# Freeing the normalised input tile by tile, earlier scores, and another split of the PSUM banks in a hybrid conv and stick-breaking attention layer

## The chip, the core and the metric

The kernel runs on one core of a Trainium2 chip. The core has five engines that run side by side and wait for each other through semaphores: TensorE (PE in the profile, its weight loads as PEld), VectorE (DVE), ScalarE (ACT), GpSimd (POOL) and SyncE (SP, which here issues the transfers between HBM and the on-chip memory). Matmul results land in PSUM, which has eight banks of 128 partitions by 512 floats; everything else sits in SBUF. The metric is the device time of one execution in microseconds (us).

## The reference

One layer over 2048 positions of 1024 channels:

```python
shift, scale, gate = jnp.split(mod[:, None, :], 3, axis=-1)
h = rms_norm(x, norm_g[l]) * (1.0 + scale) + shift
u = h @ w_in[l]
glu_in, gate_a, q, k, v, gate_b, m_a, m_b = jnp.split(u, IN_SPLITS, axis=-1)
y_a = conformer_conv_branch(glu_in, gate_a, w_dw[l], b_dw[l], ln_g[l], ln_b[l], w_conv_out[l])
q = head_rms_norm(q.reshape(bsz, seq, SB_HEADS, SB_HEAD_DIM), q_gain[l])
k = head_rms_norm(k.reshape(bsz, seq, SB_HEADS, SB_HEAD_DIM), k_gain[l])
o = stick_breaking_attention(q, k, v).reshape(bsz, seq, D_SB)
y_b = (o * jax.nn.silu(gate_b)) @ w_sb_out[l]
y = jax.nn.sigmoid(m_a) * y_a + jax.nn.sigmoid(m_b) * y_b
x = x + gate * (y @ w_out[l])
```

In the attention (8 heads of 64) a position t weighs an earlier position s by `beta[t,s]` times the product of `1 - beta[t,j]` over the positions between them, with `beta = sigmoid(q.k / 8)`. There is no softmax: the weights come from a running product along the keys.

## The kernel before

**Layout.** The host reverses the positions, so that the running product goes forward. The 2048 positions are four chunks of 512 (`NCH`, `CH`). Channels lie on the 128 partitions, so 1024 channels are eight tiles (`KC`). Each value that enters a matmul is held as a rounded high part and the remainder, and a product is three matmuls, `mm3` (high x high, high x low, low x high). A float32 weight piece of 128 x 1024 is loaded and split into its two parts by `split_into` (L99): two transfers of 512 columns through the tile `wl`, a copy on ACT, and a subtraction for the low part on POOL, or on DVE when so asked. `load_piece` puts the parts into the pool `wpa`, which has two buffers of each.

**Stages.** First the normalised input h is built for the four chunks, in the order `ORDER` = 3, 2, 1, 0, and kept in SBUF as 16 tiles a chunk (eight high, eight low; `h_tiles`, L173); the projections, the convolution and its LayerNorm follow. Queries, keys, values, gates and the branch results z (`za` from the convolution, `o` from the attention) go through HBM. Then comes the attention stage, from about 776 us on, which this document is about. The last stage multiplies z by `w_cs` (both branch projections), merges with the gates to y (`y_tiles`), multiplies by `w_out` (`out_tile`), chunk by chunk.

**The attention stage.** It runs over 80 units (h, rc, g): head, chunk of queries and chunk of keys from the diagonal on, ten for each head, four of them diagonal. One iteration of the loop takes the scores of unit u and the output of the unit before it, p, interleaved. For each of four blocks of 128 queries, Z(qb) (`z_stage`, L931) does this:

- PE: two matmuls into a PSUM bank of the pool `pz` (two banks). On a diagonal the columns that aren't needed are left out, so they are 512, 384, 256 and 256 wide.
- ACT: a sigmoid into the SBUF tile `w` (L953), then the sigmoid of the negative score over the bank itself (L954).
- DVE: the running product along the keys, a scan into `sc` (L958, or L962 on a diagonal), which reads the bank.
- POOL: the product of `w` and the shifted scan (L965), on a diagonal also a mask (L967).

The tile `w` has seven buffers (L952). For p, T(kb) (`av_stage`, L974) transposes the weights of a block of keys, one transpose for each query block (four, on a diagonal kb+1), into a PSUM tile `pT`; ACT copies its high part to `thi` (L991), DVE takes the low part `tlo` (L992), both with a priority 30 instructions ahead of their place. For the smallest diagonal block, kb = 0, 128 columns of `thi` and `tlo` are set to zero on POOL (L988, L989). AV(kb) (`av_mm`, L996) multiplies both by the values into a bank of the pool `pa` (two banks), which adds up over a row group (h, rc). When the row group is complete, ACT and DVE read the two halves of the bank out into `oc` (L1005, L1006).

Between these, `others(q, half)` puts in **fill**: the 13 remaining blocks of the merge gates, each for four chunks, in steps of one `mm3` (416 steps, `NF`, 14 of them ahead of the loop). A quarter q is a quarter of an iteration, numbered through the stage; `due` spreads the fill nearly evenly up to quarter `LAST` = 302. An output of the fill goes through a sigmoid into the tile `fsg` (two buffers, shared with `oc`) and to HBM.

The order of PE in this stage is that of the program (`pin`). On the other engines, and on SP, a scheduler fixes the order when the kernel is built, by priority, which is the place in the program, and by its own estimates.

**The changeover.** At quarter 302 the fill has ended. `hst.close()` gives back the tiles of h of all chunks as whole pools, and the pools `wr` and `yp` take their place. z of chunk 0 is loaded and split there (`load_za`, L1025, `load_zb`, L1035, through the `io` tiles), and `wcs[1]` is loaded. From quarter 307 on (`LAST + LAG`) each half quarter also does one step of `y_tiles` for chunk 0, which loads the pieces `wcs[2]` and on, two tiles ahead of their use, with the low part on DVE. The stage ends with quarter 323.

The order inside an iteration, before:

```python
Z(0); others(4 * n_, 0); av_mm(*held); others(4 * n_, 1)
Z(1); T(3); others(4 * n_ + 1, 0); T(2); others(4 * n_ + 1, 1)
Z(2); others(4 * n_ + 2, 0); AV(3); T(1); AV(2); T(0); Z(3)
others(4 * n_ + 2, 1); others(4 * n_ + 3, 0); others(4 * n_ + 3, 1); AV(1)
```

`held` is AV(0) of the iteration before.

Of the kernel before, what the change touches and what calls it, by code (L numbers as in the profile page):

```python
# [19 lines left out]
P = 128  # L20
# [31 lines left out]
def trunk_kernel(  # L52
# [115 lines left out]
    wpa = ctx.enter_context(tc.tile_pool(name="wpa", bufs=2))  # L168
    hst = ExitStack()
    hp = hst.enter_context(tc.tile_pool(name="hp", bufs=1))  # L170
    hT_ = {}

    def h_tiles(pool, g):  # L173
        hT_[g] = tuple([pool.tile([P, CH], F32R, name=f"h{p}{kc}_{g}") for kc in range(KC)]
                       for p in ("hi", "lo"))

    def hT(g):
        return hT_[g]
# [706 lines left out]
    with ExitStack() as s2:  # L885
        at = s2.enter_context(tc.tile_pool(name="at", reuse_waits="tile", bufs=1, side="right"))
        pd = s2.enter_context(tc.tile_pool(name="pd2", reuse_waits="tile", bufs=2, space=PSUM))
        pz = s2.enter_context(tc.tile_pool(name="pz", reuse_waits="tile", bufs=2, space=PSUM))
        pw = s2.enter_context(tc.tile_pool(name="pw", reuse_waits="tile", bufs=2, space=PSUM))
        pa = s2.enter_context(tc.tile_pool(name="pa", reuse_waits="tile", bufs=2, space=PSUM))  # L890
# [9 lines left out]
        def filler():  # L900

            rest = blocks[NEARLY:]
            nxt = load_piece(wpa, w_in[rest[0][0]])
            for i, (blk, dst) in enumerate(rest):
                whi, wlo = nxt
                for g in range(NCH):
                    ps = pd.tile([P, CH], F32, tag="pd", name="pd")
                    rhi, rlo = hT(g)
                    for kc in range(KC):
                        s = slice(kc * P, (kc + 1) * P)  # L910
                        mm3(ps, whi[:, s], wlo[:, s], rhi[kc], rlo[kc], kc == 0, kc == KC - 1)
                        if kc == KC - 1:
                            sg = at.tile([P, CH], F32, tag="fsg", name="fsg", bufs=2)
                            nc.scalar.activation(out=sg, in_=ps, func=AF.Sigmoid)
                            nc.sync.dma_start(dst[g], sg)
                            if g == 0 and i + 1 < len(rest):
                                nxt = load_piece(wpa, w_in[rest[i + 1][0]])
                        yield
# [55 lines left out]
        def av_stage(h, rc, g, kb, v_):  # L974
            diag = g == rc
            s_ = st[h, rc]
            if diag and kb == 3:
                s_["av"] = pa.tile([P, CH], F32, tag="av", name="av")
            av = s_["av"]
            n = (kb + 1) * P if diag else CH  # L980
            pT = pw.tile([P, CH], F32, tag="pT", name="pT")
            for qb in range(n // P):
                tr(pT[:, qb * P:(qb + 1) * P],
                                    s_["w"][g, qb][:, kb * P:(kb + 1) * P], ident)
            thi = at.tile([P, CH], F32R, tag="thi", name="thi", bufs=2)
            tlo = at.tile([P, CH], F32R, tag="tlo", name="tlo", bufs=2)
            if n == P:
                nc.gpsimd.memset(f(thi[:, P:2 * P]), 0.0)  # L988
                nc.gpsimd.memset(f(tlo[:, P:2 * P]), 0.0)  # L989
            with tc.high_priority(offset=30):  # L990
                nc.scalar.copy(out=thi[:, :n], in_=pT[:, :n])  # L991
                nc.vector.tensor_tensor(out=tlo[:, :n], in0=pT[:, :n], in1=f(thi[:, :n]),  # L992
                                        op=ALU.subtract)
            return max(n, 2 * P), av, thi, tlo
# [15 lines left out]
        wcs, wo = {}, {}  # L1010

        def resident(pool, src, name):
            hi = pool.tile([P, 1024], F32R, name=name + "h")
            lo = pool.tile([P, 1024], F32R, name=name + "l")
            split_into(src, hi, lo, nc.vector)
            return hi, lo

# [7 lines left out]
        def load_za(ch):  # L1025
            z = []
            for kc in range(JC):
                t = yp.tile([P, 2, CH], F32R, tag=f"za{kc}", name=f"za{kc}")
                o = io("n")
                nc.sync.dma_start(o, za_d[kc][ch])  # L1030
                split_z(o, t)
                z.append(t)
            return [t[:, 0, :] for t in z], [t[:, 1, :] for t in z]

        def load_zb(ch):  # L1035
            z = []
            for kc in range(JC):
                t = yp.tile([P, 2, CH], F32R, tag=f"zb{kc}", name=f"zb{kc}")
# [7 lines left out]
            return [t[:, 0, :] for t in z], [t[:, 1, :] for t in z]  # L1046

        def y_tiles(ch, za, zb, psum, y):

            for j in range(KC):  # L1050
                for i in range(2, min(KC, j + 3)):
# [42 lines left out]
        LAST = 4 * len(units) - 18  # L1094
        PRE = 14
        LAG = 5
# [15 lines left out]
        for n_, u in enumerate(units + [None]):  # L1112
# [15 lines left out]
            def others(q, half):  # L1128

                nonlocal nf, ny, ygen, wr, yp  # L1130
                while nf < (int(due[2 * q + half + 1] + 0.001) if q < LAST else NF):
                    next(fill)
                    nf += 1
                if q == LAST - 8 and not half:
                    wcs[0] = load_piece(wpa, w_cs[0])
                if q == LAST and not half:
                    hst.close()
                    wr = s3.enter_context(tc.tile_pool(name="wr", reuse_waits="tile", bufs=1))
                    yp = s3.enter_context(tc.tile_pool(name="yp", reuse_waits="tile", bufs=1))
                    with tc.high_priority(offset=0):  # L1140
                        za = load_za(0)
                        zb = load_zb(0)
                        wcs[1] = load_piece(wpa, w_cs[1])
                    ygen = y_tiles(0, za, zb, lambda n: psum(n), y)
                if q >= LAST + LAG:
# [16 lines left out]
            T(1)  # L1162
            AV(2)
            T(0)
            Z(3)
# [13 lines left out]
    with s3:  # L1179
# [3 lines left out]
        for ch in range(NCH):  # L1183
# [8 lines left out]
            for j in range(KC):  # L1192
                if ch == 0:
                    wo[j] = resident(wr if j == 0 else wor, w_out[j], f"wo{j}")
# [50 lines left out]
```

## Time and profile before

| | us |
|---|---|
| median of three runs | 1851.29 (1850.65 to 1852.08) |
| the profiled execution | 1852.87 |
| its span, first to last instruction | 1850.9 |
| attention stage in it | about 776 to 1520 |

The profile is one execution, recorded by the hardware. "Busy" of PE counts overlapping matmuls once, so a full share doesn't mean that PE is at its peak; the distance from one matmul's start to the next one's does. In a group's row stand the line, engine, operation, the tiles written and read, the shapes and the count, then the busy time, the mean length in ns and, behind the bar, the engine's idle time right before them with what ended it. In the timeline stand start, length, engine, line and operation, and in brackets the idle time before it. L118 is the helper through which every matmul goes, L123 that of the transposes; there the tiles tell them apart: `z` scores, `pT` transposes, `av` output, `pd` fill, `p` merge.

### The profile page before, as it was taken

The numbers are of one execution on the slowest core, as the hardware profiler recorded it, in microseconds if no ns is written. First come the engines' busy times: TensorE is split into PE (matmuls) and PEld (weight loads), VectorE is DVE, ScalarE is ACT, GpSimd is POOL, SyncE is SP. The second block draws the span as 40 slices with busy tenths as digits, with TensorE's granted clock in tenths as the row PEclk, the third lists the DMA queues.
The fourth block names the chain that finished last, engine by engine and source line by source line (L and its number), as shares of the span: only waits on it lengthen the run. The fifth ranks groups of instructions, "written<-read, shape, count | busy, mean of one in ns | idle before, by whom it ended". The sixth has DMA issues, their size and how long they took to land.

```text
span 1850.9 us, 27230 instructions
## 1 busy us (share of the span) xinstructions
PE 1781.9 (96%) x9612; PEld 1511.5 (82%) x9612; DVE 1232.4 (67%) x1696; ACT 825.4 (45%) x1896; POOL 668.8 (36%) x883
## 2 busy tenths in 40 slices
PE   6899999999999999999999999999999899999999
PEld 5888889899898888878777877778788677888887
DVE  7645577897879555377767777777777895334341
ACT  5465113222131134377767777767777753010100
POOL 0253112112111133266656666666666631010100
PEclk9999999999999999999999999999999999999999
DMA  8563411415032454433232323232322447353532
GB/s 285 173 189 105 138 35 54 118 47 167 28 109 91 154 188 137 158 100 95 65 98 66 102 62 106 63 98 66 100 66 89 130 144 221 108 164 98 165 97 80
DMA packets 117596, 211.08 MB, mean 114 GB/s; under 512 B 15442, under 2 KB 27730, under 8 KB 117460
## 3 DMA queue, kind: packets, MB, share of 16 engines
q1 hardware_dynamic: 116308, 207.24, 36.3%
q10 hardware_dynamic: 1152, 2.10, 0.3%
q8 instruction: 76, 1.25, 0.3%
q14 instruction: 60, 0.49, 0.1%
HBM read 137.98 MB, written 71.30 MB: 113 GB/s over the span
## 4 chain that ended last, share of the span: by engine, by line
PE 76%; DVE 7%; POOL 5%; issue 4%; ACT 4%; DMA 3%; SPq 0%; DVEq 0%; ACTq 0%; POOLq 0%
PE pd L118 43%; PE po L118 9%; PE p L118 8%; PE av L118 5%; PE pT L123 5%; PE z L118 4%; POOL w L965 3%; DVE sc L958 2%; DVE tlo L992 1%; DMA wl<-in_w_qkv_dram 1%; PE pt L123 1%; POOL wlo L106 1%; ACT z L954 1%; ACT thi L991 1%; DMA qst<-qhi 1%
## 5 line engine op out<-in xcount | busy, mean ns | idle before, releaser
L965 POOL TENSOR_TENSOR w<-w,sc 128x512 f32<-128x512 f32 (+1 forms) x320 | 361.6, 1130 | 250.2 <-DVE sc L958 178.1
L118 PE MATMUL pd<-hhi,whi 128*128 128x512 f32 x1024 | 410.9, 401 | 1.0 <-ACT vsg L871 1.0
L118 PE MATMUL pd<-hlo,whi 128*128 128x512 f32 x1024 | 399.9, 391 | 0.0
L118 PE MATMUL pd<-hhi,wlo 128*128 128x512 f32 x1024 | 399.9, 390 | 0.0
L958 DVE TENSOR_TENSOR_SCAN sc<-z,sc,w 128x512 f32<-128x512 f32 x192 | 245.0, 1280 | 90.8 <-ACT z L954 83.5
L106 POOL TENSOR_TENSOR wlo<-wl,whi 128x512 fp32r<-128x512 f32 x88 | 130.8, 1496 | 406.9 <-ACT whi L105 405.9
L953 ACT ACTIVATE w<-z 128x512 f32<-128x512 f32 (+1 forms) x320 | 172.2, 538 | 124.2 <-PE z L118 100.2
L118 PEld LDWEIGHTS pd<-hhi,wlo 128*128 128x128 f32 x1024 | 192.1, 188 | 41.9 <-POOL wlo L106 0.2
L118 PEld LDWEIGHTS pd<-hhi,whi 128*128 128x128 f32 x1024 | 194.0, 189 | 34.5 <-ACT vsg L871 1.4
L118 PEld LDWEIGHTS pd<-hlo,whi 128*128 128x128 f32 x1024 | 192.9, 188 | 33.3
L992 DVE TENSOR_TENSOR tlo<-pT,thi 128x512 fp32r<-128x512 f32 (+1 forms) x320 | 184.1, 598 | 34.4 <-ACT thi L991 31.4
L118 PE MATMUL z<-kt,q 128*128 128x512 f32 (+2 forms) x640 | 191.7, 381 | 5.6 <-DVE sc L958 4.1
L991 ACT CAST thi<-pT 128x512 fp32r<-128x512 f32 (+1 forms) x320 | 165.2, 527 | 61.6 <-PE pT L123 57.9
L123 PE MATMUL pT<-ident,w 128*128 128x128 f32 x1088 | 173.0, 274 | 10.7 <-POOL w L965 10.3
L123 PEld LDWEIGHTS pT<-ident,w 128*128 128x128 f32 x1088 | 137.1, 141 | 46.6 <-POOL w L965 15.5
L118 PE MATMUL pd<-whi,hhi 128*128 128x256 f32 x608 | 169.8, 287 | 4.3 <-ACT hhi L134 2.4
L954 ACT ACTIVATE z<-z 128x512 f32<-128x512 f32 (+1 forms) x320 | 171.9, 537 | 0.0
L118 PE MATMUL pd<-whi,hlo 128*128 128x256 f32 x608 | 166.9, 285 | 0.9 <-POOL u L654 0.6
L118 PE MATMUL pd<-wlo,hhi 128*128 128x256 f32 x608 | 154.3, 284 | 0.0
L962 DVE TENSOR_TENSOR_SCAN sc<-z,tri 128x512 f32<-128x512 f32 (+3 forms) x128 | 104.4, 819 | 60.1 <-ACT z L954 42.0
L118 PE MATMUL av<-tlo,vt 128*128 128x512 f32 (+1 forms) x320 | 123.0, 384 | 14.0 <-DVE tlo L992 10.6
L118 PEld LDWEIGHTS z<-kt,q 128*128 128x128 f32 x640 | 109.3, 189 | 24.3 <-DVE sc L958 6.9
(284 smaller groups left out, 3109.8 us busy)
## 6 DMA issues: line engine op xcount, KB each, us to landing
wl<-in_w_in_dram SPq DMA_DIRECT2D x64, 256.0 KB, 2.9
wa<-in_w_ada_dram SPq DMA_DIRECT2D x24, 512.0 KB, 4.9
wl<-in_w_qkv_dram SPq DMA_DIRECT2D x36, 256.0 KB, 2.8
xt<-in_x_n_dram SPq DMA_DIRECT2D x16, 512.0 KB, 5.8
vst<-st SPq DMA_DIRECT2D x64, 128.0 KB, 2.1
kt<-kst SPq DMA_DIRECT2D x32, 256.0 KB, 2.8
vt<-vst SPq DMA_DIRECT2D x32, 256.0 KB, 2.7
q<-qst SPq DMA_DIRECT2D x32, 256.0 KB, 2.8
```

The source lines that it names most:

```text
L106: (lo_eng or nc.gpsimd).tensor_tensor(out=lo[:, s], in0=wl, in1=f(hi[:, s]), op=ALU.subtract)
L118: i = nc.tensor.matmul(*a, **k)
L123: i = nc.tensor.transpose(*a)
L953: nc.scalar.activation(out=w[:, lo:], in_=z[:, lo:], func=AF.Sigmoid, scale=HD ** -0.5)
L954: nc.scalar.activation(out=z[:, lo:], in_=z[:, lo:], func=AF.Sigmoid, scale=-HD ** -0.5)
L958: nc.vector.tensor_tensor_scan(out=s[:, 1:], data0=z, data1=w, initial=s[:, 0:1], op0=ALU.mult, op1=ALU.bypass)
L962: nc.vector.tensor_tensor_scan(out=s[:, lo + 1:], data0=z[:, lo:], data1=tri[:, :CH - lo], initial=1.0, op0=ALU.mult, op1=ALU.max)
L965: nc.gpsimd.tensor_tensor(out=w[:, lo:], in0=w[:, lo:], in1=s[:, lo:CH], op=ALU.mult)
L991: nc.scalar.copy(out=thi[:, :n], in_=pT[:, :n])
L992: nc.vector.tensor_tensor(out=tlo[:, :n], in0=pT[:, :n], in1=f(thi[:, :n]), op=ALU.subtract)
```

## The change

- Of h, the tiles of chunks 3 and 2 come to lie in two pools of their own, X and Y, with high and low part of a channel tile in one tile. Each is given back by itself when its last reader is done.
- The last two blocks of the fill are done for chunks 3 and 2 first, and for chunks 0 and 1 after that. So X and Y are not read any more from 32 steps before the end of the fill.
- From there on z of chunk 0 goes into X (`z0`) and the pieces `wcs[1]` to `wcs[4]` go into Y (`in_place`), one in two quarters, 60 instructions behind their place in priority. The attention half of z follows from quarter 302 on. z of later chunks uses X as well.
- The fill is spread up to quarter 307 (`LAST`), and the merge steps begin there at once, without the five quarters between. `wo[0]` is loaded at that point.
- Z(3) moves from behind T(0) to ahead of AV(2).
- `pz` has three banks, `pa` one.
- The zeros of the smallest diagonal block are written by ACT.

```diff
     wpa = ctx.enter_context(tc.tile_pool(name="wpa", bufs=2))
+
+    hx_ = [ctx.enter_context(tc.tile_pool(name=f"hp{n}", reuse_waits="tile", bufs=1))
+           for n in "XY"]
...
+    def pair_tile(n, kc, name):
+
+        return hx_[n].tile([P, 2, CH], F32R, tag=f"c{kc}", name=name)
+
     def h_tiles(pool, g):
+        if g in ORDER[:2]:
+            t = [pair_tile(ORDER.index(g), kc, f"hh{kc}") for kc in range(KC)]
+            hT_[g] = tuple([a[:, i, :] for a in t] for i in range(2))
+            return
...
-        pz = s2.enter_context(tc.tile_pool(name="pz", reuse_waits="tile", bufs=2, space=PSUM))
+        pz = s2.enter_context(tc.tile_pool(name="pz", reuse_waits="tile", bufs=3, space=PSUM))
...
-        pa = s2.enter_context(tc.tile_pool(name="pa", reuse_waits="tile", bufs=2, space=PSUM))
+        pa = s2.enter_context(tc.tile_pool(name="pa", reuse_waits="tile", bufs=1, space=PSUM))
...
+            n = len(rest)
+            seq = [(i, g) for i in range(n - 2) for g in range(NCH)]
+
+            for gs in (ORDER[:2], ORDER[:1:-1]):
+                seq += [(i, g) for i in (n - 2, n - 1) for g in gs]
...
             if n == P:
-                nc.gpsimd.memset(f(thi[:, P:2 * P]), 0.0)
-                nc.gpsimd.memset(f(tlo[:, P:2 * P]), 0.0)
+                nc.scalar.mul(thi[:, P:2 * P], ident, 0.0)
+                nc.scalar.mul(tlo[:, P:2 * P], ident, 0.0)
...
+        def in_place(i):
+
+            hi, lo = (pair_tile(1, 2 * (i - 1) + k, "wcx").rearrange("p t c -> p (t c)")
+                      for k in range(2))
+            split_into(w_cs[i], hi, lo, nc.vector)
+            wcs[i] = hi, lo
+
+        def z0(kc):
+
+            t = pair_tile(0, kc, "z0")
+            nc.sync.dma_start(f(t[:, 1, :]), (za_d + o_d)[kc][0])
+            raw = f(t[:, 1, :])
+            if kc >= JC:
+                nc.sync.dma_start(f(t[:, 0, :]), gb_d[kc - JC][0])
+                raw = at.tile([P, CH], F32, tag="fsg", name="zo", bufs=2)
+                nc.gpsimd.tensor_tensor(out=raw, in0=f(t[:, 1, :]), in1=f(t[:, 0, :]),
+                                        op=ALU.mult)
+            nc.scalar.copy(out=t[:, 0, :], in_=raw)
+            nc.vector.tensor_tensor(out=t[:, 1, :], in0=raw, in1=f(t[:, 0, :]),
+                                    op=ALU.subtract)
+            zt[kc] = t
...
-                for i in range(2, min(KC, j + 3)):
+                for i in range(5, min(KC, j + 4)):
...
-        LAST = 4 * len(units) - 18
+        LAST = 4 * len(units) - 13
         PRE = 14
-        LAG = 5
+
+        FREE = NF - 4 * KC
+        early = [(FREE, 0, f_, a) for f_, a in ((z0, 0), (in_place, 1), (z0, 1), (in_place, 2),
+                                                (z0, 2), (z0, 3), (in_place, 3), (in_place, 4))]
+        early += [(NF, 4 * len(units) - 18 + k + k // 3, z0, JC + k) for k in range(JC)]
...
+                if early and not half:
+                    steps, quarter, f_, a = early[0]
+                    if (nf >= steps and q % 2 == 0) if quarter == 0 else q >= quarter:
+                        early.pop(0)
+
+                        with tc.high_priority(offset=-60):
+                            f_(a)
...
                     with tc.high_priority(offset=0):
-                        za = load_za(0)
-                        zb = load_zb(0)
-                        wcs[1] = load_piece(wpa, w_cs[1])
-                    ygen = y_tiles(0, za, zb, lambda n: psum(n), y)
-                if q >= LAST + LAG:
+                        wo[0] = load_piece(wpa, w_out[0])
+                    z0_ = [zt[kc] for kc in range(2 * JC)]
+                    ygen = y_tiles(0, halves(z0_[:JC]), halves(z0_[JC:]), lambda n: psum(n), y)
+                if q >= LAST:
                     next(ygen)
...
             AV(3)
             T(1)
+            Z(3)
             AV(2)
             T(0)
-            Z(3)
```

More of the change, by code (lines that the diff above doesn't have):

```diff
@@ L902, in filler @@
             rest = blocks[NEARLY:]
[L903 to L918, printed above, removed]
+            n = len(rest)
+            seq = [(i, g) for i in range(n - 2) for g in range(NCH)]
+            for gs in (ORDER[:2], ORDER[:1:-1]):
+                seq += [(i, g) for i in (n - 2, n - 1) for g in gs]
+            w = [load_piece(wpa, w_in[rest[0][0]])]
+            for k, (i, g) in enumerate(seq):
+                ps = pd.tile([P, CH], F32, tag="pd", name="pd")
+                rhi, rlo = hT(g)
+                whi, wlo = w[i]
+                if i == n - 2 == len(w) - 1:
+                    w.append(load_piece(wpa, w_in[rest[i + 1][0]]))
+                for kc in range(KC):
+                    s = slice(kc * P, (kc + 1) * P)
+                    mm3(ps, whi[:, s], wlo[:, s], rhi[kc], rlo[kc], kc == 0, kc == KC - 1)
+                    if kc == KC - 1:
+                        sg = at.tile([P, CH], F32, tag="fsg", name="fsg", bufs=2)
+                        nc.scalar.activation(out=sg, in_=ps, func=AF.Sigmoid)
+                        nc.sync.dma_start(rest[i][1][g], sg)
+                        if i == len(w) - 1 and len(w) < n:
+                            w.append(load_piece(wpa, w_in[rest[i + 1][0]]))
+                    yield
         kt, vt = {}, {}
@@ L1007, in av_mm @@
                 nc.sync.dma_start(o_d[h // 2][rc][a], oc[a])
-        wcs, wo = {}, {}
+        wcs, wo, zt = {}, {}, {}
         def resident(pool, src, name):
@@ L1016, in resident, with halves @@
             return hi, lo
+        def in_place(i):
[16 more added lines that the diff above has]
+            zt[kc] = t
+        def halves(t):
+            return [a[:, 0, :] for a in t], [a[:, 1, :] for a in t]
         def io(name):
@@ L1027, in load_za @@
             for kc in range(JC):
-                t = yp.tile([P, 2, CH], F32R, tag=f"za{kc}", name=f"za{kc}")
+                t = pair_tile(0, kc, f"za{kc}")
                 o = io("n")
@@ L1032, in load_za @@
                 z.append(t)
-            return [t[:, 0, :] for t in z], [t[:, 1, :] for t in z]
+            return halves(z)
         def load_zb(ch):
@@ L1037, in load_zb @@
             for kc in range(JC):
-                t = yp.tile([P, 2, CH], F32R, tag=f"zb{kc}", name=f"zb{kc}")
+                t = pair_tile(0, JC + kc, f"zb{kc}")
                 o = io("o")
@@ L1045, in load_zb @@
                 z.append(t)
-            return [t[:, 0, :] for t in z], [t[:, 1, :] for t in z]
+            return halves(z)
         def y_tiles(ch, za, zb, psum, y):
             for j in range(KC):
-                for i in range(2, min(KC, j + 3)):
+                for i in range(5, min(KC, j + 4)):
                     if i not in wcs:
@@ L1136, in others @@
                 if q == LAST and not half:
+                    assert not early
                     hst.close()
@@ L1192, in trunk_kernel @@
             for j in range(KC):
-                if ch == 0:
-                    wo[j] = resident(wr if j == 0 else wor, w_out[j], f"wo{j}")
+                if ch == 0 and j:
+                    wo[j] = resident(wor, w_out[j], f"wo{j}")
                 out_tile(ch, j, y, psum)
```

## The prediction

> **What bounds the kernel now.** I read the sums by window first, then the groups by shape, the waits, and last the timeline of single units.
>
> ```profile
> span 1850.9 us, 27230 instructions
> ```
>
> ```profile
> 776.00:1455.00 679.00, 657.47 (x3459) 539.11 (x3460) 498.56 (x626) 482.04 (x1007) 436.21 (x691) 1.00 0.28 85
> 1455.00:1520.00 65.00, 54.94 (x261) 41.35 (x260) 59.72 (x81) 42.89 (x89) 38.83 (x48) 0.97 0.54 164
> 1520.00:1550.00 30.00, 28.90 (x127) 23.33 (x126) 22.19 (x35) 13.13 (x22) 0.00 (x0) 1.00 0.72 214
> 1550.00:1851.00 301.00, 297.03 (x1311) 245.57 (x1309) 107.62 (x152) 29.08 (x47) 16.27 (x12) 1.00 0.42 126
> ```
>
> Columns: stretch, length, busy of PE, PEld, DVE, ACT, POOL, granted clock, DMA share, GB/s. The attention stage runs to 1520 us; from 1455 us on is the changeover, where the fill is used up and the merge of chunk 0 begins. PE is what has to be filled: after 1550 us it works nearly all the time, so only the stage before has something to give. In the changeover PE idles 10 of 65 us while DVE is 92% busy.
>
> Busy PE time hides more, since matmuls overlap. The true step comes from stretches where nothing waits (the chain of waits: start, length, what, count), the amount of work from the groups by shape:
>
> ```profile
> 1448.11 0.44 PE pT L123 x4
> ...
> 1585.91 43.52 PE p L118 x192
> ```
>
> ```profile
> L123 PE MATMUL pT<-ident,w 128*128 128x128 f32 x1088 | 173.0, 274 | 10.7 <-POOL w L965 10.3 <-POOL w L967 0.3
> L118 PE MATMUL pd<-hhi,whi 128*128 128x512 f32 x416 | 172.0, 414 | 1.0 <-ACT vsg L871 1.0
> ...
> L118 PE MATMUL z<-kt,q 128*128 128x512 f32 x448 | 146.0, 407 | 3.0 <-DVE sc L958 2.5 <-ACT w L953 0.5
> ...
> L118 PE MATMUL av<-tlo,vt 128*128 128x512 f32 x224 | 92.0, 411 | 2.5 <-DVE tlo L992 2.2
> ...
> L118 PE MATMUL av<-tlo,vt 128*128 128x384 f32 x32 | 12.7, 397 | 8.5 <-DVE tlo L992 8.3
> ```
>
> A 512-wide matmul steps every 43.52/192 = 0.227 us, a transpose every 0.11. From 776 to 1520 us stand 3x416 fill, 448 score, 2x224 output and 102 merge matmuls of 512 (34 merge steps of three; 2246 in all, 510 us), 1088 transposes (120 us), and by the loops of the code 128 of 384 and 256 of 256 (by width about 22 and 29 us): 681 us of work in 744. **About 63 us are lost**, which is the most that can be won there.
>
> Where PE waited between 780 and 1450 us (total, times, longest):
>
> ```profile
> PEld av L118 <- DVE tlo L992: 21.7, 46, 1.0
> ...
> PEld pT L123 <- POOL w L965: 12.5, 19, 1.6
> PE av L118 <- DVE tlo L992: 9.0, 18, 0.7
> PE pT L123 <- POOL w L965: 8.0, 18, 1.4
> ...
> PE av L118 <- POOL tlo L989: 2.9, 2, 1.5
> ...
> PE z L118 <- DVE sc L962: 0.8, 1, 0.8
> ```
>
> Two waits matter: the output matmul for tlo, and T(3)'s last transpose for the weights of the last query block. A score bank is hardly waited for (0.8).
>
> **Part by part.**
>
> *Last scores up, the output.* Z(3) moves ahead of AV(2) and T(0). In a unit whose weights belong to a diagonal block:
>
> ```profile
> 1100.97 0.42 PE L118 MATMUL av<-thi,vt 128*128 128x384 f32 x1
> ...
> 1102.14 0.45 PE L118 MATMUL av<-tlo,vt 128*128 128x384 f32 x1 [0.75 <-DVE tlo L992]
> ```
>
> AV(2) stands idle 0.75 us for tlo; Z(3), 2x0.227 = 0.45 us of PE work that follows anyhow, now fills the hole. Only AV(2) of a diagonal unit is 384 wide, so the 8.3 us of its group are this wait alone. Each is cut by up to 0.45 (by half of that where the scores are 256 wide): **-7 us**. Bounds: 0, and -12 with the wide units that PEld shows waiting too.
>
> *Last scores up, the weights.* Z(3) feeds ACT, ACT again, the scan, POOL, then T(3) of the next unit:
>
> ```profile
> 1111.23 0.60 PE L123 MATMUL pT<-ident,w 128*128 128x128 f32 x4
> 1111.59 0.71 PE L118 MATMUL z<-kt,q 128*128 128x512 f32 x2
> 1111.87 0.59 ACT L991 CAST thi<-pT 128x512 fp32r<-128x512 f32 x1 [0.31 <-PE pT L123]
> ...
> 1112.35 0.60 ACT L953 ACTIVATE w<-z 128x512 f32<-128x512 f32 x1
> ...
> 1112.84 0.61 ACT L954 ACTIVATE z<-z 128x512 f32<-128x512 f32 x1
> ...
> 1113.55 1.28 DVE L958 TENSOR_TENSOR_SCAN sc<-z,sc,w 128x512 f32<-128x512 f32 x1
> ...
> 1114.92 1.28 POOL L965 TENSOR_TENSOR w<-w,sc 128x512 f32<-128x512 f32 x1 [1.24 <-DVE sc L958]
> ...
> 1115.93 1.09 PE L123 MATMUL pT<-ident,w 128*128 128x128 f32 x8
> ```
>
> T(3)'s last transpose starts as POOL ends (1116.20), so scores 0.9 us earlier look like the end of that wait. But L952 gives w seven buffers. At Z(3) four hold the previous unit's weights and three the present one's; the eighth is free when T(0), their last reader, has read its first block. Before, Z(3) stood behind T(0) and never met this. Now its first activation waits for T(0), however early the scores are; behind it on ACT stand the second activation and the copies thi, and AV waits for those. In these rows T(0) moves by Z(3)'s 0.45 to 1111.68, its first transpose is done 0.27 later, and w starts near 1112.0 instead of 1112.35. By then T(0) is nearly through, and its copy thi has the higher priority (offset 30). What ACT does in such a place Z(1) shows, with the copies of T(3) and T(2):
>
> ```profile
> 1107.38 0.60 ACT L953 ACTIVATE w<-z 128x512 f32<-128x512 f32 x1 [0.99 <-PE z L118]
> 1107.87 1.07 ACT L991 CAST thi<-pT 128x512 fp32r<-128x512 f32 x2
> 1108.81 0.62 ACT L954 ACTIVATE z<-z 128x512 f32<-128x512 f32 x1
> ```
>
> The copies went between the two activations. Steps of 0.49 and 0.54 there; so with one copy z starts at 1112.0 + 0.49 + 0.54 = 1113.03, 0.2 later than now; with none, at 1112.49, 0.35 earlier. T(3) keeps its place. The order is fixed when the kernel is built and this trace can't show it; I take the copy in between, as at Z(1), and its 0.2 us in the 19 units that wait already: **+4 us**. Bounds: -8 (the wait is gone) and +28 (a copy of 0.59 ahead of both activations in all 48 units whose last block has full width).
>
> *Three score banks, one for the output.* The third bank makes Z(3)'s new place possible; by itself it wins 0.8 us before the changeover, counted as 0. One output bank adds a wait: AV(3) of a new row group needs the old sum read out, 32 times, and all of PE stands behind it. The tightest place:
>
> ```profile
> 1099.03 0.69 DVE L1006 TENSOR_TENSOR oc<-av,oc 64x512 f32<-64x512 f32 x1
> ...
> 1100.12 0.39 PE L118 MATMUL av<-thi,vt 128*128 128x512 f32 x1
> ```
>
> 0.40 us are left. **+1 us**; bounds 0 and +28 (oc one scan later everywhere, 32x(1.28-0.40)).
>
> *Zeros from POOL to ACT.* 64 fills leave POOL for ACT, which is 71% busy (482 of 679). An ACT operation of full width takes 0.59 in the rows above, so 128 columns take less; only AV(0) of the next unit reads them. PE's wait for POOL's zeros goes: **-3 us**; bounds -3 and, with every fill at 0.27 (the transpose's length, as a stand-in) on ACT's chain, +17. I take the near end because of ACT's gaps.
>
> *Changeover.* Before, the fill ends at quarter 302; for five quarters PE has attention alone, exposed to its chain, while z and weights are loaded and split:
>
> ```profile
> 1455.88 1.02 SPq L1030 DMA_DIRECT2D n<-za  x2
> ...
> 1461.91 0.73 PE L118 MATMUL z<-kt,q 128*128 128x512 f32 x2 [1.25 <-DVE sc L958]
> ...
> 1468.69 0.63 PE L118 MATMUL p<-za,whi 128*128 128x512 f32 x2
> ```
>
> ```profile
> 1465.00:1470.00 5.00, 5.00 (x22) 3.88 (x21) 4.04 (x6) 3.60 (x8) 3.66 (x4) 0.73 0.56 137
> ```
>
> After, the last four fill items use chunks 0 and 1 only; X and Y are free 32 steps before the end (about quarter 283), and the loads of z and of four weight pieces go there, one in two quarters, at low priority. Their issues pass SP, where the loads of q, k and v stand behind them, but they wait only for tiles whose readers are done; I count 0 for SP (it costs a late q otherwise). The 402 steps are spread over 307 quarters instead of 302: no PE work is added, the five bare quarters are covered, and the clock dip (5 us at 0.73) goes. What is late next is DVE:
>
> ```profile
> 1415.00:1520.00 105.00, 94.23 (x469) 73.79 (x468) 89.30 (x116) 71.77 (x146) 62.52 (x87) 0.98 0.39 118
> ```
>
> DVE's 89 us stay (the pieces' low halves are on DVE in both, one piece more now). Even at 97% they need 92, so at most 13 us can go. I take **-9 us**, bounds -13 and 0: 1.3 for the clock, the rest the bare quarters.
>
> Sum: -7 + 4 + 1 - 3 - 9 = **-14 us**. The profiled execution took 1852.87 us, 2.0 of it outside its span; the runs' median is 1851.29, and the difference goes on the median: **1837 us**.
>
> **A rule against the early loads.** The low halves are subtractions out of SBUF, moved into a stretch where POOL works:
>
> ```profile
> L106 DVE TENSOR_TENSOR wc4l<-wl,wc4h 128x512 fp32r<-128x512 f32 x2 | 3.0, 1515 | 0.0
> ...
> L106 DVE TENSOR_TENSOR wc6l<-wl,wc6h 128x512 fp32r<-128x512 f32 x2 | 1.4, 702 | 0.1
> ```
>
> The same operation took 1.5 us in the changeover and 0.7 after it, where POOL has no instruction (the window from 1520). Eight of them at 0.8 more are 6.5 us of DVE, where DVE is last to end. The Trainium skill, page "SBUF — State Buffer", section "Who interferes with whom", says that a DVE instruction with two SBUF inputs contends with a GpSimd instruction that reads SBUF; by that rule, which the two lengths agree with, the eight meet POOL's products and the sum would be -14 + 6.5, near 1844 us.
>
> **The rivals.**
> 1. *z follows w at once, no copy between*, as at Z(3) in the rows above. Against: the copy outranks it and is ready. T(3)'s wait goes, -8 in place of +4: 1825 us.
> 2. *The changeover saves nothing*: DVE stays the last to end, with the dearer subtractions. For it: 92% busy there. -14 + 9 = -5: 1846 us.
> 3. *Slower: ACT held at its head.* If Z(3)'s first activation waits for its buffer so that a copy (0.59 us) goes ahead of the whole chain, 48 units pay 48x0.59 = 28 us instead of 4: -14 - 4 + 28 = +10, 1861 us. The other terms give 18, so it decides from 18/48 = 0.38 us a unit. For it: T(3) has no slack in the rows. Against: ACT has gaps, and a stall of PE lets the others catch up.
>
> **Chances.** Forecast 0.45, rivals 0.28, 0.15 and 0.12. This kernel's measurement tells about 0.2% from no change, 3.7 us. Faster: forecast, first rival, and the second for a third of it, 0.78; within 0.11; slower 0.11. The range takes in the first two rivals and the bounds about them: 1818 to 1853.
>
> **What would show it.** The 384-wide AV(2) waits under 3 us; no wait for zeros; Z(3)'s first activation starts with T(0)'s first transpose, and T(3) still waits for POOL's weights (if not, rival 1); a changeover without a clock dip. I am wrong if the stage before it doesn't shrink, if AV(3) waits for oc, or if DVE subtractions of 1.5 us stand under T(3)'s waits.

## The result, and the profile after

| | us |
|---|---|
| before, median of 6 runs on the same chips | 1852.16 (1850.65 to 1853.80) |
| after, median of 6 runs | 1839.89 (1838.47 to 1840.99) |
| ratio, 95% interval | 0.9937 [0.9927, 0.9947] |
| forecast | 1837 (1818 to 1853) |

The change makes the kernel 12.3 us faster, where 14 had been forecast. The profiled execution after took 1840.99 us.

The head of the page of after, then its sums for three stretches of the attention stage. They are cut where the same iteration of the loop begins in every kernel: at iteration 66 (quarter 264) and iteration 76 (quarter 304). Columns as in the prediction.

```profile
span 1839.3 us, 27219 instructions
```

```profile
780.00:1352.60 572.60, 564.99 (x2988) 464.42 (x2987) 435.45 (x549) 427.87 (x931) 372.45 (x551) 1.00 0.29 89
1352.60:1449.70 97.10, 87.76 (x457) 70.39 (x456) 79.57 (x98) 70.86 (x154) 60.66 (x83) 1.00 0.39 120
1449.70:1507.00 57.30, 50.44 (x257) 40.17 (x257) 48.05 (x63) 33.97 (x74) 29.80 (x38) 1.00 0.34 102
```

The same three stretches of before:

```profile
780.00:1372.40 592.40, 572.30 (x3010) 468.81 (x3009) 436.68 (x549) 421.65 (x880) 380.56 (x603) 1.00 0.28 87
1372.40:1459.50 87.10, 84.72 (x452) 69.58 (x450) 66.21 (x84) 63.72 (x134) 55.60 (x88) 1.00 0.26 79
1459.50:1520.00 60.50, 51.56 (x244) 38.91 (x245) 55.39 (x75) 38.92 (x80) 35.49 (x45) 0.97 0.54 162
```

PE's idle time is the length less its busy time: 20.1, 2.4 and 8.9 us before, 7.6, 9.3 and 6.9 after. The loop ahead of the changeover gained; the middle stretch, where after now loads z and weights, lost; the last one, with the fill up to its end, gained a little, and the clock dip (0.97) is gone.

Idle time misses what a matmul loses while another still runs, so I use a finer measure below, the **lost time**: from one matmul's start to the next one's, less the step that it takes where nothing waits (0.2265 us at 512 columns, 0.172 at 384, 0.118 at 256, 0.109 for a transpose), summed over the stage's 3718 matmuls and put down to the group that started late. The work so counted is equal in both kernels; only the loss differs:

| lost us | loop, to quarter 264 | 264 to 304 | from 304 | sum |
|---|---|---|---|---|
| before | 43.0 | 5.7 | 15.7 | 64.4 |
| after | 28.2 | 14.3 | 9.8 | 52.3 |

That is -14.8, +8.6, -5.9: 12.1 us less in the stage, whose length from first to last matmul went from 743.74 to 731.74. Ahead of the stage 0.95 us went, behind it 1.3 came; the span is 11.6 shorter.

In the loop, the waits of PE, before (780 to 1372.4 us) and after (780 to 1352.6); total, times, longest:

```profile
PE av L118 <- DVE tlo L992: 8.4, 17, 0.7
PE pT L123 <- POOL w L965: 7.3, 15, 1.4
PE av L118 <- POOL tlo L989: 2.9, 2, 1.5
PE z L118 <- DVE sc L962: 0.8, 1, 0.8
```

```profile
PE av L118 <- DVE tlo L1009: 3.4, 10, 0.8
PE pT L123 <- POOL w L982: 2.6, 5, 0.9
```

The wait for tlo fell by 5.0, that for the weights by 4.7, those for the zeros and for a score bank are gone. By place the lost time of the loop went from 12.7 to 6.1 at AV(2), 3.5 to 0 at AV(0), 3.9 to 2.3 at T(0), 1.4 to 0.4 at Z(2); T(3) only from 12.8 to 11.5, and AV(3) stayed (3.7 and 3.6). How the slow steps right behind a late start are shared out moves these figures by place: put down strictly to the matmul that starts late, AV(2) goes from 10.2 to 4.3, T(3) from 10.8 to 9.1 and T(0) from 2.7 to 1.7, while the sums of the stretches stay. So a difference at one place is good to about 1.5 us, here and below. The group of the 384-wide AV(2) over the stage, after:

```profile
L118 PE MATMUL av<-tlo,vt 128*128 128x384 f32 x32 | 12.7, 396 | 2.3 <-DVE tlo L1009 2.1
```

It waited 8.3 us for tlo before, 2.1 now.

T(3)'s loss stands in the trace at the place that the prediction named. The timeline of ACT in after, at a Z(3):

```profile
1100.52 0.60 ACT L970 ACTIVATE w<-z 128x512 f32<-128x512 f32 x1 [0.40 <-PE pT L123]
1101.01 0.58 ACT L1008 CAST thi<-pT 128x512 fp32r<-128x512 f32 x1
1101.48 0.61 ACT L971 ACTIVATE z<-z 128x512 f32<-128x512 f32 x1
```

The first activation waited for T(0), as in 22 of the 48 units whose last block has full width, and the copy thi stands between it and the second one, as in all 48.

### The profile page after: what moved, and what is told of

The parts are those of the page before. It is cut to its first block, busy times and chain, and to the rows that moved or that the text cites. A ratio compares the mean times of both kernels' runs of the same rounds, so it can differ in the third digit from the quotient of the medians.

```text
span 1839.3 us, 27219 instructions
## 1 busy us (share of the span) xinstructions
PE 1777.6 (97%) x9612; PEld 1510.2 (82%) x9612; DVE 1233.2 (67%) x1696; ACT 833.5 (45%) x1960; POOL 658.7 (36%) x819
## 4 chain that ended last, share of the span: by engine, by line
PE 75%; DVE 7%; DMA 5%; POOL 4%; issue 4%; ACT 4%; SPq 1%; DVEq 0%; ACTq 0%; POOLq 0%
PE pd L118 43%; PE po L118 8%; PE p L118 8%; PE av L118 5%; PE pT L123 5%; PE z L118 5%; POOL w L982 2%; DVE sc L975 2%; DVE tlo L1009 1%; DMA wl<-in_w_qkv_dram 1%; ACT z L971 1%; POOL wlo L106 1%; PE pt L123 1%; DMA qst<-qhi 1%; DMA xt<-in_x_n_dram 1%
## 5 line engine op out<-in xcount | busy, mean ns | idle before, releaser
L118 PE MATMUL pd<-hh,whi 128*128 128x512 f32 x1024 | 325.8, 399 | 0.0
L118 PEld LDWEIGHTS pd<-hh,whi 128*128 128x128 f32 x1024 | 184.2, 190 | 31.4
L118 PE MATMUL pd<-hhi,whi 128*128 128x512 f32 x512 | 208.5, 407 | 1.0 <-ACT vsg L882 1.0
L118 PE MATMUL pd<-hh,wlo 128*128 128x512 f32 x512 | 200.3, 391 | 0.0
L118 PE MATMUL pd<-hhi,wlo 128*128 128x512 f32 x512 | 200.2, 391 | 0.0
L118 PE MATMUL pd<-hlo,whi 128*128 128x512 f32 x512 | 200.2, 391 | 0.0
L118 PE MATMUL av<-tlo,vt 128*128 128x512 f32 (+1 forms) x320 | 121.0, 378 | 11.1 <-DVE tlo L1009 10.4
L105 ACT CAST whi<-wl 128x512 fp32r<-128x512 f32 x88 | 53.6, 622 | 163.2 <-PE pd L118 135.5
L118 PE MATMUL av<-thi,vt 128*128 128x512 f32 (+1 forms) x320 | 116.7, 365 | 0.8 <-ACT thi L1008 0.8
L1116 ACT CAST yh<-ma 128x512 fp32r<-128x512 f32 x32 | 19.9, 621 | 206.4 <-DVE ma L1113 206.4
```

The costliest lines, as they stand in the source:

```text
L105: nc.scalar.copy(out=hi[:, s], in_=wl)
L118: i = nc.tensor.matmul(*a, **k)
L1116: nc.scalar.copy(out=hi, in_=ma)
```

## The experiments

Two groups of runs take the change apart, a third looks for something better. The expectations name theories by letters; each says what it expects. Each time is a median, with that of the kernel before in the same runs behind it. No run leaves out any work.

### The loop part alone, and the changeover alone

**e1_loop_only**: the kernel before with Z(3) early, three banks and one, the zeros on ACT.

```diff
-  pz bufs=2, pa bufs=2
+  pz bufs=3, pa bufs=1
-  nc.gpsimd.memset(f(thi[:, P:2 * P]), 0.0)
+  nc.scalar.mul(thi[:, P:2 * P], ident, 0.0)
   T(1)
+  Z(3)
   AV(2)
   T(0)
-  Z(3)
```

> The kernel before with the loop's part of the change alone: Z(3) ahead of AV(2) and T(0), three score banks and one output bank, zeros on ACT; the changeover as before. Theory A (the trace of the changed kernel: the stage up to quarter 280 gets 14.6 us shorter, of which 4 are fill that moved behind it, and what follows gets 2.6 us longer): the loop is the whole gain, so about 10 us faster than before, 1842, give or take 3. Rival B (the prediction's split): the loop gives 5 and the changeover 9, so about 1847. Rival C: the early Z(3) costs more in the bare changeover, where nothing covers PE's chain, and the gain is under 3 us.

1841.02 against 1851.04, ratio 0.9946 [0.9933, 0.9960]: theory A's value. Lost time 29.5, 3.3 and 20.7 us in the three stretches.

**e2_changeover_only**: after, with these edits undone.

```diff
-  pz bufs=3, pa bufs=1
+  pz bufs=2, pa bufs=2
-  nc.scalar.mul(thi[:, P:2 * P], ident, 0.0)
+  nc.gpsimd.memset(f(thi[:, P:2 * P]), 0.0)
-  Z(3)
   AV(2)
   T(0)
+  Z(3)
```

> The changed kernel with Z(3) back behind T(0), two banks for scores and two for outputs, zeros on POOL: the changeover's part of the change alone. Theory A: it is worth nearly nothing by itself, 0 to -3 us against before (1849 to 1852), because the splits moved ahead make T(3) wait for POOL's weights in quarters 283 to 307 for as long as the bare quarters cost. Rival B: -9 us, 1843. Rival C: slower than before, since score banks are waited for.

1847.42 against 1851.04, 0.9977 [0.9968, 0.9987]; lost 39.0, 11.1 and 9.2. The loop part by itself brings 10.0 us, the changeover by itself 3.6. Together they bring 12.3, and the intervals of e1 and after overlap: that the new changeover adds anything to the early scores isn't shown.

What it does there can be read off. From e1 to after the last stretch loses 10.9 us less (20.7 to 9.8): this is the cover of the bare quarters that the prediction counted on, together with the lower clock of e1 there (its row stands further down). The middle stretch loses 11.0 more (3.3 to 14.3), and what was gained is spent. The last run of the study tells the spread of the fill from the rest.

**e12_thinner_fill**: e1 with the fill spread to quarter 307, and the merge still five quarters behind it, so that ten steps of the merge move behind the stage.

```diff
-  LAST = 4 * len(units) - 18
+  LAST = 4 * len(units) - 13
```

> The loop-only kernel with one number changed: the fill spread up to quarter 307 for 302, the old changeover five quarters later with it. About 4 us of fill leave the quarters ahead of 280. Theory A (with the early scores the loop waits for its chain through ACT, DVE and POOL, and fill only covers that wait): the stretch from the stage's start to quarter 280, 617.1 us in the loop-only kernel, shrinks by 1 us or less, while PE's lost time in it grows by 3 to 4; the whole is 0 to 4 us slower than the loop-only kernel, 1841 to 1845, as fewer quarters are left to overlap with the merge. Rival B (PE's work binds): the stretch shrinks by the 4 us that left it, to 613. Rival C: both by about half.

1841.41 against 1851.36, 0.9940 [0.9926, 0.9953]; lost 28.3, 3.4 and 18.2. From the stage's start to quarter 280 it took 612.2 us against 617.1 in e1: 4.9 less, as B had it. The idea that the loop is bound by its chain, and that less fill only means more waiting, is refuted. To quarter 264, e12 and after take the same time (577.5 and 577.4 us); then they part. Sums of e12:

```profile
1353.70:1439.80 86.10, 85.58 (x457) 70.48 (x456) 66.68 (x85) 64.91 (x141) 55.22 (x83) 1.00 0.24 74
1439.80:1498.70 58.90, 49.59 (x227) 38.80 (x226) 48.09 (x67) 38.81 (x82) 34.22 (x38) 0.88 0.52 160
```

The middle stretch has the same 457 matmuls in both, and takes 86.1 us in e12, 97.1 in after. What after has more there is 13 DVE instructions and 12.9 us of DVE, the subtractions of the early z and of the weight pieces, and the 13 copies on ACT that go with them (154 instructions for 141). The waits of PE in this stretch, in after and then in e12:

```profile
PE pT L123 <- POOL w L982: 4.6, 4, 1.8
PE av L118 <- DVE tlo L1009: 4.5, 8, 1.1
```

```profile
PE av L118 <- DVE tlo L992: 0.3, 1, 0.3
```

DVE is still only 82% busy (79.57 of 97.10), so its share doesn't tell where these waits come from; the timeline does. DVE, POOL and PE of after:

```profile
1374.01 0.66 DVE L1023 TENSOR_TENSOR oc<-av,oc 64x512 f32<-64x512 f32 x1
1374.59 1.82 DVE L1053 TENSOR_TENSOR z<-z 128x512 fp32r<-128x512 f32 x1
1376.33 0.68 DVE L1009 TENSOR_TENSOR tlo<-pT,thi 128x512 fp32r<-128x512 f32 x1
```

```profile
1374.17 1.69 POOL L982 TENSOR_TENSOR w<-w,sc 128x512 f32<-128x512 f32 x1 [3.33 <-DVE sc L975]
```

```profile
1375.57 0.39 PE L118 MATMUL av<-thi,vt 128*128 128x512 f32 x1
1377.06 0.50 PE L118 MATMUL av<-tlo,vt 128*128 128x512 f32 x1 [1.10 <-DVE tlo L1009]
```

This is iteration 68. A subtraction of z stands ahead of tlo and takes 1.82 us, and AV(3) waits 1.10 for tlo. In the next iteration two more of them stand ahead of a scan:

```profile
1383.12 2.33 DVE L1053 TENSOR_TENSOR z<-z 128x512 fp32r<-128x512 f32 x2
```

```profile
1383.27 1.63 POOL L982 TENSOR_TENSOR w<-w,sc 128x512 f32<-128x512 f32 x1 [2.01 <-DVE sc L975]
```

```profile
1384.95 0.33 PE L123 MATMUL pT<-ident,w 128*128 128x128 f32 x1 [1.77 <-POOL w L982]
```

This POOL product is lengthened too (1.63, where one that meets no subtraction takes 1.28), and T(3) waits 1.77 for it. By iteration, those with a lengthened subtraction (68, 69, 71 and 72) lose 8.8 of the 10.9 us that the ten iterations of this stretch lose more than in e12. Iteration 70, with two of 0.7 us, loses 0.3; 73 and 74, without one, 1.2. The waits stand behind the subtractions on the timeline, but no run leaves out the subtractions alone: the copies on ACT came forward with them, and AV(0) waited for one of these once.

### The loop part, edit by edit

All are after with one edit taken back or changed.

**e5_scores_at_old_place**: `Z(3)` behind `T(0)` again, the banks left as changed.

```diff
-  Z(3)
   AV(2)
   T(0)
+  Z(3)
```

> The changed kernel with Z(3) back behind T(0), all else as changed. Theory A (the early scores fill the hole ahead of AV(2)): the wait of AV(2) comes back, 5 to 7 us, T(3)'s wait stays as it is, and the time is 5 to 7 us above the changed kernel, about 1846. Rival B (the early scores also shorten T(3)'s wait): 10 us or more above it. Rival C: nothing changes, since another wait takes AV(2)'s place.

1847.04 against 1851.6, 0.9973 [0.9963, 0.9984], some 7 us slower than after. AV(2)'s loss in the loop is back at 12.7 (6.1), T(3)'s is 13.6 (11.5). e2, with this changeover and the old banks and zeros, took 1847.42: at the old place of Z(3) the third bank and the zeros on ACT together bring nothing that the time shows.

**e7_banks_two_two**: early scores with the old banks.

```diff
-  pz bufs=3, pa bufs=1
+  pz bufs=2, pa bufs=2
```

> The changed kernel with two banks for scores and two for a head's output, Z(3) still early. Theory A: the third bank is what Z(3)'s place needs: PE waits at Z(3) for the scan of Z(1), ahead of AV(2) and T(0), 0.2 to 0.4 us in most units, 10 to 20 us, so 1850 to 1860. Rival B: the scan is done by then in most units and the time stays within 3 us of 1840. Rival C: faster by 2 or more, as the second output bank takes AV(3)'s wait for the read-out away.

1849.85 against 1851.6, 0.9986 [0.9978, 0.9995]. The scores now wait for the bank that the scan of Z(1) reads; waits of e7 in the loop:

```profile
PE z L118 <- DVE sc L975: 7.1, 18, 0.9
```

```profile
PEld z L118 <- DVE sc L975: 14.1, 27, 1.1
```

So the place of Z(3) and the third bank are one edit in two halves: without the banks some 9 us are lost again, without the place some 7.

**e6_zeros_on_pool**:

```diff
-  nc.scalar.mul(thi[:, P:2 * P], ident, 0.0)
+  nc.gpsimd.memset(f(thi[:, P:2 * P]), 0.0)
```

> The changed kernel with the zeros written by POOL again. Theory A: AV(0)'s wait for the zeros comes back, 3 us in two or three places, so 1842 to 1843. Rival B: the zeros cost ACT as much as POOL, and the time is the same within 1.5 us. Rival C: faster by 2 or more, since 64 operations leave ACT, on which the chain to T(3) runs.

1842.26 against 1851.6, 0.9949 [0.9937, 0.9962]: about 2 us slower than after in the medians, but the intervals overlap, so the time alone doesn't show it. The trace does show the wait: AV(0) loses 5.8 us in the loop where it lost none.

**e3_copy_after_scores**: the copies of kb = 0 lose their priority, so that none stands between Z(3)'s activations.

```diff
-  with tc.high_priority(offset=30):
+  with tc.high_priority(offset=30 if kb else 0):
```

> The changed kernel with one edit: the copy and the remainder for kb = 0 have no raised priority, so that in the built order no copy stands between the two activations of Z(3) (48 units had one). Theory A: the weights of Z(3) are ready 0.54 us earlier, and T(3)'s wait for POOL (about 0.25 us in each of 48 units) mostly goes: 8 to 12 us faster than the changed kernel, about 1830. Rival B: T(3)'s wait only moves to AV(0) or AV(1), whose copy is later now, and the time stays within 3 us of 1840. Rival C: slower by 5 or more, as the output chain is the tighter one.

1840.7 against 1851.04, 0.9939 [0.9927, 0.9952]: no difference, as B said. T(3)'s loss in the loop goes from 11.5 to 3.5 us, and AV(0), which needs the copy, loses 7.5 where it lost none. The copy between is no mistake of the order; either one or the other waits.

**e4_eight_w**: an eighth buffer for w, so that Z(3) needn't wait for T(0); paid for with one buffer less in the tag `fsg`.

```diff
-  tag="w", bufs=7
-  tag="fsg", bufs=2
+  tag="w", bufs=8
+  tag="fsg", bufs=1
```

> The changed kernel with eight buffers of w for seven, and one for two of the staging tile fsg to make room for it. Theory A: the first activation of Z(3) waits for the score matmul and no more for T(0); in 25 of 48 units the copy also goes out from between. T(3)'s wait goes in most units: 8 to 12 us faster than the changed kernel, 1828 to 1832, less what the single staging tile costs (ACT waits for a transfer of some 2 us where fill and output meet, a few times: 0 to 3 us). Rival B: the buffer isn't what binds, DVE is, and the time stays within 3 us of 1840. Rival C: the single staging tile costs more than the buffer gives, 1845 or more.

1848.76 against 1851.04, 0.9983 [0.9974, 0.9992], as C said. T(3) loses less (6.5), AV(3) much more (13.8 for 3.6). One row of its waits in the loop says why:

```profile
PE av L118 <- DVE oc L1023: 6.4, 4, 2.0
```

With one staging tile, oc has to wait its turn with the gates, and with one output bank AV(3) waits for oc. The theory that w's seventh buffer holds T(3) is supported by T(3)'s loss alone; what an eighth buffer is worth without this price wasn't tried, for want of room.

### Looking for a better order

**e8_t0_ahead_of_av2**: T(0) goes ahead of AV(2) too, so that its transposes free w and fill the wait for tlo.

```diff
   Z(3)
-  AV(2)
   T(0)
+  AV(2)
```

> The changed kernel with T(0) ahead of AV(2), so T(1), Z(3), T(0), AV(2). T(0) needs the transposed tile that AV(2)'s remainder frees, which AV(2) needs too, so PE waits no longer there; and the seventh buffer's successor comes free 0.45 us earlier, while the copy of T(0) has to wait for AV(2) and stands between the activations in 25 units only. Theory A: the weights of Z(3) are ready 0.45 to 1 us earlier, T(3)'s wait of 21 us falls by half or more without a later AV(0): 8 to 12 us faster than the changed kernel, 1828 to 1832. Rival B: as in the run with the copy behind the scores, the wait moves to AV(0), AV(3) or AV(1), and the time stays within 3 us of 1840. Rival C: slower, T(0) waits longer than AV(2) did.

1835.96 against 1851.6, 0.9917 [0.9903, 0.9931]: some 4 us faster than the change in the medians, at most half of what A hoped for, and the intervals still overlap a little (that of after begins at 0.9927). In the loop T(3) loses 5.4 for 11.5 and AV(2) 2.7 for 6.1, but T(0) 7.7 for 2.3. Waits of e8 in the loop:

```profile
PE pT L123 <- DVE tlo L1009: 3.6, 11, 0.4
PE av L118 <- DVE tlo L1009: 2.1, 4, 0.7
PE pT L123 <- POOL w L982: 1.1, 2, 0.8
```

The transposes now wait until tlo has been taken out of their PSUM tile.

**e9_t0_first_old_changeover**: the same edit on e1.

```diff
   Z(3)
-  AV(2)
   T(0)
+  AV(2)
```

> The kernel before with the loop's part of the change and T(0) ahead of AV(2); the changeover as before. With the changed changeover this order took 1836. Theory A (the changeover's part gains where the bare quarters are exposed, and gives most of it back in T(3)'s waits ahead of them): 1836 to 1838. Rival B (with the better order of the loop the changeover is worth what it was worth alone, 4 us or more): 1840 or more. Rival C: the changeover costs, and this is faster than 1834.

1838.19 against 1851.73, 0.9926 [0.9914, 0.9939]; lost 28.8, 3.6 and 17.9. The order seems to help without the new changeover as well: 2.8 us less than e1, with intervals that overlap a little. What e8 has beyond it is again within the intervals.

**e10_low_parts_on_pool**: e8, with the low parts of the pieces in Y taken on POOL.

```diff
-  split_into(w_cs[i], hi, lo, nc.vector)
+  split_into(w_cs[i], hi, lo)
```

> The changed kernel with T(0) ahead of AV(2), and the low parts of the four early weight pieces on POOL for DVE: eight subtractions of 0.66 to 1.7 us leave DVE, which is the last to end in T(3)'s longer waits of quarters 284 to 307, and take 1.3 us each on POOL, which is busy two thirds there. Theory A (DVE binds in that stretch): the waits of T(3) from quarter 280 on, 6.4 us, fall by 2 to 4, about 1833. Rival B (POOL's product for the next T(3) is what binds): they stand behind POOL's products now, and the time is 2 to 5 longer, 1838 to 1841. Rival C: no difference beyond 1.5 us.

1836.61 against 1851.73, 0.9914 [0.9901, 0.9928]: no difference from e8. In the middle stretch T(3) loses 2.1 for 4.7, AV(3) 4.5 for 1.7: with eight splits off DVE the loss moves and doesn't go.

**e11_early_loads_spread**: e8, with three of the four tiles of the attention half of z among the early loads.

```diff
-  (z0, 2), (z0, 3), (in_place, 3), (in_place, 4))]
+  (z0, JC), (in_place, 3), (z0, JC + 1), (z0, 2),
+  (in_place, 4), (z0, JC + 2), (z0, 3))]
-  early += [(NF, 4 * len(units) - 18 + k + k // 3, z0, JC + k) for k in range(JC)]
+  early += [(NF, 4 * len(units) - 14, z0, 2 * JC - 1)]
```

> The changed kernel with T(0) ahead of AV(2), and the attention half of z for the first six heads mixed into the early list (eleven steps in quarters 284 to 304 and the last at 306, in place of eight steps to quarter 299 and four in 302 to 306). Theory A (the bunch of POOL products, copies and subtractions in quarters 302 to 306 makes the longest wait of T(3), 2.6 us, and its neighbours): 2 to 4 us faster than 1836. Rival B (the amount of work of DVE and POOL in the stretch counts, not its bunching): within 1.5 us of 1836. Rival C: slower, since more transfers stand ahead of the loads of k and q on SP.

1835.53 against 1851.73, 0.9911 [0.9897, 0.9924], within 1.5 us of e8. The last stretch loses 6.5 for 9.6, the middle one 13.2 for 12.6. It is the fastest of the runs, and its interval lies below that of after: 16.2 us less than the kernel before, some 4 to 5 less than the change.

## Why the prediction came out right, and where it was wrong

The sum was right, -14 against -12.3 in the medians. Its two parts were not, and their errors nearly cancel, so it is luck that the number came out this near. By place in the trace, **the loop gave 14.8 us where 5 were forecast, the changeover cost 2.7 where 9 were to be won.**

| term | forecast | measured, lost us |
|---|---|---|
| AV(2), wait for tlo | -7 | -6.6 |
| T(3), wait for the weights | +4 | -1.3 (e1: +0.4) |
| one output bank | +1 | -0.1 at AV(3) |
| zeros on ACT | -3 | -3.5 at AV(0) |
| T(0), Z(2) and other places of the loop | 0 | -3.3 |
| changeover, from quarter 264 on | -9 | +2.7 |
| behind the stage | 0 | +1.3 |
| ahead of the stage | 0 | -1.0 |

- **AV(2)**: mechanism and size hold. e5 puts the loss back (12.7), the 384-wide group fell to 2.3 us of idle time.
- **T(3)**: the mechanism holds: first activation with T(0), copy between. The size was off. I charged 0.2 us to each of 19 units, and the loss in the loop hardly moved. The bounds reached from -8 to +28, and e3 shows why neither end came: the order of the copy only decides whether T(3) or AV(0) waits.
- **Banks**: right that a third bank makes the new place possible; e7 shows it, at some 9 us. Counting the bank "by itself" as 0 holds (e5 has it and no gain from it at AV(2)). No wait for oc came with two staging tiles.
- **Zeros**: right at AV(0), where 3.5 us of lost time went; the 2 us of e6 lie within the intervals.
- **Places left out**: T(0) and Z(2) lost 2.6 us less. The old score wait (0.8 in its row) stood for 1.0 of this, and a T(0) that no longer runs straight behind AV(2)'s wait starts less late. Only the first is in the rows; the second is argued.
- **Changeover**, the step that failed: "no PE work is added, the five bare quarters are covered", with DVE's 89 us kept as a cap on the gain. The cover came, the dip went (-5.9 in the last stretch from before, -10.9 from e1). But I added up DVE's time and didn't ask where in an iteration the moved subtractions would stand. Of the twelve in iterations 68 to 72, each ahead of a tlo or a scan or of another of them, six take 1.49 to 1.82 us, and the iterations with these pay most of the +11.0. "At low priority" was no cover: the first of them stands at 1374.59, in iteration 68 (quarters 272 to 275), ahead of quarter 283, and AV(3) and T(3) stood behind them. That the early loads and splits cost this is shown by after and e12, whose matmuls in the stretch are the same; that it is their DVE part alone is read off the timeline, and e10, where eight went to POOL for no gain, doesn't support it. What the early issues cost on SP, put at 0, no run tells apart.

A last +2.6 us stands in the changeover of e1 already: it loses 24.0 from quarter 264 on, before 21.4, all of it in the bare stretch (20.7 for 15.7, with the middle one better). Whether the early scores cause it is open, since the clock of e1 is lower there. Its sums:

```profile
1440.60:1506.10 65.50, 53.94 (x246) 42.17 (x245) 62.87 (x77) 41.20 (x89) 36.33 (x40) 0.90 0.51 161
```

A clock of 0.90 over 65.5 us lacks 6.6 us, that of before (0.97 over 60.5) 1.8: by this estimate the clock alone could make nearly all of the difference of 5.0, and up to 6.6 of the 10.9 us that after gains on e1 there. Why e2's loop loses 4 us less than that of before is open; the fill is thinner there, but the built order differs as well.

**The rivals.** The first fell: a copy stands between. The third fell: Z(3)'s first activation is held by T(0), but no copy goes ahead of it, and T(3)'s loss didn't grow. The second, that the changeover saves nothing because of dearer subtractions, is what happened there by place (alone, in e2, the new changeover still gains 3.6); its 1846 missed because the loop gave more. Of the signs named, those of the loop came as said, as did a changeover without a dip, and so did the one that was to prove me wrong: subtractions under T(3)'s waits (1383.12).

**The rule against the early loads.** The Trainium skill, page "SBUF — State Buffer", section "Who interferes with whom", lets a DVE instruction with two SBUF inputs contend with a GpSimd instruction that reads SBUF. The trace agrees. The groups of DVE in after, 1375 to 1510 us:

```profile
L106 DVE TENSOR_TENSOR wcx<-wl,wcx 128x512 fp32r<-128x512 f32 x8 | 8.1, 1010 | 0.2 <-ACT wcx L105 0.2
L1053 DVE TENSOR_TENSOR z<-z 128x512 fp32r<-128x512 f32 x4 | 5.9, 1484 | 0.0
L1053 DVE TENSOR_TENSOR z<-zo,z 128x512 fp32r<-128x512 f32 x4 | 4.3, 1074 | 2.8 <-ACT z L1052 2.7
...
L106 DVE TENSOR_TENSOR wc6l<-wl,wc6h 128x512 fp32r<-128x512 f32 x2 | 1.4, 688 | 0.3 <-ACT wc6h L105 0.3
```

At 0.69 us each, the sixteen of the first three rows would be 11.0 us; they took 18.3. That is 7.3 more, where the prediction had 6.5 for eight of them; but the eight of the weight pieces took only 2.6 more, those of z the rest. And before pays part of this too: in its changeover the eight of z and the six of wc2 to wc4 took 13.7 us, 4.0 above 0.69 each. So the move added about 3 us of DVE time. By the rule the changeover would have won 2.5 us, nearer to the measured +2.7 than the -9 was; its sum of 1844 is 4 us too high, since the loop gave more.

One reading under the rule was wrong. The two wc6l subtractions of before, 0.70 us on average, did not run after 1520 us where POOL is idle, but at 1508.74 and 1511.64. DVE and POOL of before:

```profile
1508.74 0.66 DVE L106 TENSOR_TENSOR wc6l<-wl,wc6h 128x512 fp32r<-128x512 f32 x1
```

```profile
1508.90 1.10 POOL L965 TENSOR_TENSOR w<-w,sc 128x256 f32<-128x256 f32 x1 [0.53 <-DVE sc L962]
```

The first met a product of POOL and kept its length. So not every subtraction beside a product gets longer; the last section goes into it.

## What to carry to other kernels

Work that is moved under a cover has a price on every engine of the chain beside it: look where in the iteration its instructions will stand on the engine that feeds the next wait, not at that engine's busy share (82% here, and 11 us lost). An early issue and the buffer that it needs are one edit, and each half alone can be worth nothing (e5, e7). After an edit to an order, add up the lost time by place: a wait that goes from one place and turns up at another (e3, e4, e10) leaves the time as it was, or makes it worse.

## What the runs showed of the hardware that I had not expected

The prediction took a subtraction beside POOL's product to be slower. In most pairs of the trace the two take turns. DVE and POOL of after, two pairs 6 us apart:

```profile
1406.38 1.55 DVE L106 TENSOR_TENSOR wcx<-wl,wcx 128x512 fp32r<-128x512 f32 x1
...
1412.34 0.66 DVE L106 TENSOR_TENSOR wcx<-wl,wcx 128x512 fp32r<-128x512 f32 x1
```

```profile
1406.08 1.29 POOL L982 TENSOR_TENSOR w<-w,sc 128x512 f32<-128x512 f32 x1 [0.81 <-DVE sc L975]
...
1412.50 1.62 POOL L982 TENSOR_TENSOR w<-w,sc 128x512 f32<-128x512 f32 x1 [1.43 <-DVE sc L975]
```

In the first pair POOL began first, kept its 1.29 us and ended at 1407.37; the subtraction ended 0.56 later. In the second DVE began first and kept its 0.66; the product ended 1.12 us behind it. The ends come out the same in all 13 overlapping pairs of such a subtraction and a product of full width in this stage of after: the one that starts second ends 0.54 to 0.56 us (DVE, eleven pairs) or 1.12 us (POOL, two pairs) behind the end of the first, whatever the overlap. But the one that starts first doesn't always keep its length. The product at 1374.17 above took 1.69 us though it began 0.42 ahead of its subtraction, and in e11, where one began 0.41 ahead, the subtraction kept its length and POOL paid. DVE and POOL of e11:

```profile
1373.93 0.68 DVE L1053 TENSOR_TENSOR z<-z 128x512 fp32r<-128x512 f32 x1
```

```profile
1373.52 2.24 POOL L982 TENSOR_TENSOR w<-w,sc 128x512 f32<-128x512 f32 x1 [3.52 <-DVE sc L975]
```

What decides between the two there is open. A tlo, which reads PSUM and SBUF, keeps its length beside a product (0.66 to 0.69 us in all 213 of full width that overlap one). DVE and POOL of after:

```profile
1404.14 0.67 DVE L1009 TENSOR_TENSOR tlo<-pT,thi 128x512 fp32r<-128x512 f32 x1
```

```profile
1403.72 1.29 POOL L982 TENSOR_TENSOR w<-w,sc 128x512 f32<-128x512 f32 x1 [2.07 <-DVE sc L975]
```

So the price of such a subtraction depends on the moment at which it starts, and POOL can be the one that pays it.
